# A two-layer decoder trunk on one core: all heads in each step of the recurrence, and the key projection moved between the steps

## Chip, cores and metric

One Trainium2 chip, one core. The metric is the device time of one execution in microseconds (us). Engines: TensorE (PE, its weight loads PEld), VectorE (DVE), ScalarE (ACT), GpSimd (POOL) and SyncE (SP), whose queue issues most of the DMA transfers.

## What is computed

A residual stream of 2048 tokens by 1024 channels passes an RWKV-7 layer (layer A, 16 heads of 64), then one shared key and value projection, then a dilated attention layer (layer B). Cut to what matters here:

```
xr = xr + gate * rwkv7(modulated(rms(xr)))            # layer A: wkv7 state, one per head
kv = rms(xr, kv_norm_g) @ w_kv                        # D -> 2D
k_sh = rope(rms(kv[..., :D] per head, k_norm_g)); v_sh = kv[..., D:]
h = rms(xr, b_norm_g) * (1 + scale) + shift           # layer B's modulated input
q (3 groups), gate = h @ w_in                         # D -> 4D
xr = xr + gate_b * (attention(rope(rms(q)), k_sh, v_sh) * silu(gate)) @ w_out
```

with the state of a head, per token: `state = state*w + (state·a) b^T + v k^T`, `y = state·r`.

## The kernel before, in words

Matrices are multiplied to f32 accuracy in three passes (`mm3`, L68 to 76): both operands are split into a high and a low f32r half, and high·high, high·low and low·high are accumulated. So a projection matmul is three instructions, on L72, L73 and L74.

`phase1` (to 1084 us) computes layer A's projections and writes what the recurrence needs to scratch in HBM. `phase2` (L797 to 1180) runs the recurrence in 32 chunks of 64 tokens. `loads` (L847) fetches a chunk's operands on SP's queue; `prep` (L869) makes the next chunk's matrices on TensorE (L881, L894, L903, L910) with evacuations on ACT and DVE; `chain` (L930) is the serial part. It has three matmul steps with an evacuation behind each: L942 (with L944, a part of the output `y`), evacuated to `qc` by `evac` (L925); L959, evacuated into the state tile `x`; L965 (with L967, the rest of `y`), which DVE scales (`up`, L973) and adds (L976) to make the next chunk's state. A chunk's 16 heads go in two halves `hb`, each a generator of its own, and the loop over chunks (L1150 on) calls the two in turn, so that one half's matmuls stand where the other half's evacuation runs. The L-numbers of these lines are those of the profile; a source matmul in f32 shows as two records there.

Work that fills the time between the steps is kept in a list `work` and advanced by `slot` (L1128): each of a chunk's ten slots advances `prep`, the group norm of the chunk before, and one yield of `work` (two from chunk 24 on if more than one is queued). `work` holds the output projection `out_proj` (L1056) of a block of 256 tokens (every four chunks): 192 matmuls of 256 columns, layer A's result `x1T` to HBM, its sum of squares, and at the end (L1093 to 1096) `rstd1`, the reciprocal root that the norms of the shared key/value and of layer B use. `spread` ties each filler matmul behind the `LAG`-th last mark of the recurrence, `yielding` the DVE work likewise (`DLAG`); the rest of the order is set by a scheduler.

`phase3` runs dense jobs in the order of `JOBS`: `k`, `v`, the queries `2`, `1`, `0`, then `gate` and `out`. A job is 256 places of three matmuls of 512 columns (8 token blocks, 2 halves, 2 groups of 128 tokens, 8 pieces of the contraction). `tokens` (L1296) loads a piece of `x1T` and splits it; in job `v` it also makes layer B's modulated input (`rstd`, L1317, `modulated`) and writes it to `xbT`, which the query jobs read. `rotated` (L1448) norms and rotates keys or queries (`rms_rope`, L1198), transposes them (L1457) and stores them, the keys twice (`K1` and `K2`). Attention starts behind job `2` (`tick(256 * 3 + 14)`).

## Time and profile before

| | us |
|---|---|
| median of 3 runs (3877.28 to 3890.25) | 3888.3 |
| the profiled execution | 3889.0 |
| its span, first to last instruction | 3887.1 |
| recurrence, first to last step | 1086 to 1839 |
| rest of layer A's output projection | 1839 to 1896 |
| jobs `k`, `v`, `2` | 1896 to 2122, to 2313, to 2522 |
| rest (queries 1 and 0, gate, attention, output) | 2522 to 3887 |

TensorE is busy 3700.6 us of the span (95%), DVE 2494.7, ACT 1822.1, POOL 1430.8; the mean granted TensorE clock is 0.962 of full speed. A busy TensorE is one with a matmul in flight, not one at its peak: how densely matmuls start is read from the timeline, from start to start.

### The profile page before, as it was taken

The page shows a single profiled execution, that of the slowest core. Times are in us where ns is not written, and L with a number is a line of the kernel's source. Part 1 is how long each engine was busy: PE and PEld are TensorE (multiplying, and loading weights), DVE is VectorE, ACT ScalarE, POOL GpSimd, SP SyncE. Part 2 cuts the span into 40 slices and gives each one's busy share as a digit, 9 for nine tenths or more (in the row PEclk, how much of TensorE's full clock was granted, in tenths as well). Part 3 has the DMA queues.
Part 4 walks back from the last instruction along what each step waited for, and adds up shares of the span by engine and source line. Part 5 has one row for each costly group of instructions (what it writes and reads, how often), then busy time and mean ns, then how long its engine had stood idle before and what let it go on. Part 6 is the DMA issues. An engine that isn't in the chain of part 4 may idle for free.

```text
span 3887.1 us, 79932 instructions
## 1 busy us (share of the span) xinstructions
PE 3700.6 (95%) x29328; PEld 2930.5 (75%) x29328; DVE 2494.7 (64%) x6213; ACT 1822.1 (47%) x4734; POOL 1430.8 (37%) x1377
## 2 busy tenths in 40 slices
PE   7899999999989999999898999999999999999999
PEld 5565667767777888888776877777777788887888
DVE  4884477889866565465576347777876664455556
ACT  4554443343334443344444233456666665565441
POOL 3341355564344343333344234533432220023232
PEclk9899999999979998899999999999999999999999
DMA  9774467675665443343578455665655565456655
GB/s 279 224 242 138 131 181 205 175 211 163 175 134 124 99 111 90 89 109 92 135 124 167 138 160 79 118 144 144 183 149 136 134 171 138 148 168 193 188 165 174
DMA packets 1027128, 595.31 MB, mean 153 GB/s; under 512 B 564912, under 2 KB 918576, under 8 KB 1020592
## 3 DMA queue, kind: packets, MB, share of 16 engines
q1 hardware_dynamic: 629040, 500.00, 46.1%
q10 hardware_dynamic: 397696, 90.20, 11.1%
q8 instruction: 232, 3.80, 0.4%
q14 instruction: 160, 1.31, 0.1%
HBM read 391.84 MB, written 198.18 MB: 152 GB/s over the span
## 4 chain that ended last, share of the span: by engine, by line
PE 69%; DVE 12%; DMA 7%; issue 4%; POOL 4%; ACT 2%; SPq 1%; ACTq 0%; DVEq 0%; POOLq 0%
PE ps L72 12%; PE ps L74 11%; PE ps L73 11%; PE sc L1640 4%; PE z L881 4%; PE pv L1672 4%; PE z L1661 3%; PE pd L72 2%; PE pd L73 2%; DVE q L1215 2%; PE pd L74 1%; POOL rr_st L1207 1%; DMA bk<-bkD 1%; PE z L269 1%; PE ps L942 1%
## 5 line engine op out<-in xcount | busy, mean ns | idle before, releaser
L1652 ACT ACTIVATE yt<-yt,nm 128x256 f32<-128x256 f32 (+1 forms) x768 | 345.1, 450 | 294.6 <-DVE nm L1648 293.8
L72 PE MATMUL ps<-xh,wh 128*128 128x512 f32 (+1 forms) x1248 | 449.7, 369 | 7.2 <-ACT xh L358 5.6
L73 PE MATMUL ps<-xl,wh 128*128 128x512 f32 (+1 forms) x1248 | 448.0, 360 | 5.4 <-DVE xl L360 4.0
L74 PE MATMUL ps<-xh,wl 128*128 128x512 f32 (+1 forms) x1248 | 445.1, 358 | 0.0
L72 PE MATMUL ps<-xh 128*128 128x512 f32 (+1 forms) x1152 | 419.1, 364 | 4.3 <-ACT ov L1485 2.8
L74 PE MATMUL ps<-xh,xl 128*128 128x512 f32 (+1 forms) x1152 | 400.4, 348 | 0.0
L73 PE MATMUL ps<-xl,xh 128*128 128x512 f32 (+1 forms) x1152 | 398.5, 346 | 0.0
L1207 POOL TENSOR_TENSOR rr_st<-rr_st,mh 128x8 f32<-128x8 f32 x128 | 215.6, 1684 | 469.6 <-DVE rr_st L1206 411.4
L74 PE MATMUL ps<-wh,xl 128*128 128x512 f32 x896 | 362.8, 407 | 14.4 <-DVE xl L66 13.8
L72 PE MATMUL ps<-wh,xh 128*128 128x512 f32 x896 | 370.8, 415 | 4.8 <-ACT q L1450 1.7
L73 PE MATMUL ps<-wl,xh 128*128 128x512 f32 x896 | 361.2, 403 | 0.7 <-DVE wl L1286 0.6
L72 PEld LDWEIGHTS ps<-xh,wh 128*128 128x128 f32 x1248 | 238.9, 193 | 81.3 <-issue 35.8
L1645 DVE CUSTOM_DVE_ANT_0 yt<-sc,amask 128x256 f32<-128x256 f32 (+1 forms) x768 | 237.2, 360 | 86.6 <-PE sc L1640 80.5
L73 PEld LDWEIGHTS ps<-xl,wh 128*128 128x128 f32 x1248 | 240.3, 193 | 60.7 <-issue 18.2
L74 PEld LDWEIGHTS ps<-xh,wl 128*128 128x128 f32 x1248 | 240.4, 193 | 51.6 <-issue 22.2
L72 PEld LDWEIGHTS ps<-xh 128*128 128x128 f32 x1152 | 218.0, 189 | 50.9 <-issue 19.0
L74 PEld LDWEIGHTS ps<-xh,xl 128*128 128x128 f32 x1152 | 217.8, 189 | 27.7 <-issue 0.3
L73 PEld LDWEIGHTS ps<-xl,xh 128*128 128x128 f32 x1152 | 218.5, 190 | 23.0 <-issue 0.3
L1212 POOL TENSOR_TENSOR rr_a<-rr_sq,TCS 128x512 f32<-128x512 f32 x128 | 183.4, 1433 | 114.4 <-DVE rr_sq L1210 98.0
L278 DVE SCALAR_TENSOR_TENSOR t<-hx,vecs,t 128x512 f32<-128x512 f32 x192 | 170.5, 908 | 81.9 <-ACT t L277 81.6
L1215 DVE TENSOR_TENSOR q<-rr_sq,TCS 128x256 f32<-128x256 f32 x256 | 219.7, 898 | 2.6
L74 PEld LDWEIGHTS ps<-wh,xl 128*128 128x128 f32 x896 | 172.0, 192 | 63.9 <-DVE xl L66 26.3
(341 smaller groups left out, 8830.7 us busy)
## 6 DMA issues: line engine op xcount, KB each, us to landing
hx<-hT SPq DMA_DIRECT2D x152, 256.5 KB
xb<-xbT SPq DMA_DIRECT2D x256, 128.0 KB
x<-Q SPq DMA_DIRECT2D x96, 256.0 KB
kq<-K SPq DMA_DIRECT2D x72, 256.0 KB
st<-in_w_in SPq DMA_DIRECT2D x64, 256.0 KB
arD<-ar SPq DMA_DIRECT2D x32, 512.0 KB
bkD<-bk SPq DMA_DIRECT2D x32, 512.0 KB
ls<-arD SPq DMA_DIRECT2D x64, 256.0 KB
```

The lines of the kernel that those rows point to most:

```text
L72: i = mm(out, lh, rh, start=first, stop=False, **kw)
L73: mm(out, lh, rl, start=False, stop=False, **kw)
L74: mm(out, ll, rh, start=False, stop=last, **kw)
L278: nc.vector.scalar_tensor_tensor(t1, hx[:, 0:512], self.vec["a_mix_mu"][:, m:m + 1], t1, op0=ALU.mult, op1=ALU.add)
L881: mm(at[s][:, j], bk[rows[s], 4 * hb + j].rearrange("p a t -> p (a t)"), ls1[b][rows[s], s, 4 * hb + j].rearrange("p a t -> p (a t)"), sta ...
L1207: nc.gpsimd.tensor_tensor(st[:, 1], st[:, 0], mh, op=ALU.pow)
L1212: nc.gpsimd.tensor_tensor(a, sq, TC[:, tt, None, :].to_broadcast([P, 8, 64]), op=ALU.mult)
L1215: nc.vector.tensor_tensor(v[:, :, lo:lo + 32], sq[:, :, hi:hi + 32], TS[:, tt, None, lo:lo + 32].to_broadcast([P, 8, 32]), op=ALU.mult)
L1640: j = mm(sc[h][:, x, :u.n * P], qt[r, c], kq[r, k1 - u.n * P:k1], start=True, stop=True)
L1645: nc.vector.tensor_tensor_reduce(out=u.pr[:, h, :nk], in0=sc[h][:, x, :nk], in1=amask[:, int(g == 0), 256 - nk:256], scale=1.0, scalar=-3e ...
L1652: nc.scalar.activation(u.pr[:, h, :nk], u.pr[:, h, :nk], AF.Exp, bias=nm[:, x, h:h + 1], accum_out=lm[:, x, h, 0:1])
L1672: prev[0] = self.after(mm(pv[e, u.i], u.vt[:, u.i + 2 - u.n + kb, e], u.pts[:, h, kb], start=(kb == 0), stop=(kb == u.n - 1)), prev[0])
```

## The change

The chain takes all heads in each step, in one PSUM bank for each; the two generators become one. The chunk keeps ten slots, now behind the four yields of `SLOTS`, and each advances `work` by two yields (three late). Behind each block's `out_proj`, `keys(v)` is queued: it loads the block's `x1T` back, makes the modulated input and writes it to `xbT` (scale on POOL, affine on ACT), and makes the raw key projection, which goes to `kraw`. Block 0 splits the key weights and stores both halves in `wkD`; blocks 1 to 7 load both halves from there, 32 transfers of 256 KB each. `phase3` loses job `k`; the keys are loaded from `kraw` and rotated in job `v`, and `tokens` no longer modulates. The operand tile `bk` gets a second buffer.

```diff
-LAG = 3
-DLAG = 4
+LAG = 2
+DLAG = 2
...
+SLOTS = (3, 3, 3, 1)
...
+        self.xbT = self.scratch("xbT", (D, T))
+        self.kraw = self.scratch("kraw", (T, D))
+        wkD = self.scratch("wkD", (2 * KC, 2, P, 512))
...
-            bp, ep, lp, kp = pool("bp", 1, cctx), pool("ep", 1, cctx), pool("lp", 2, cctx), pool("kp", 1, cctx)
+            bp, ep, lp, kp = pool("bp", 2, cctx), pool("ep", 1, cctx), pool("lp", 2, cctx), pool("kp", 1, cctx)
...
-            for n, bufs in (("wst", 2), ("dp", 1), ("op", 2)):
+            for n, bufs in (("wst", 2), ("dp", 1), ("op", 2), ("wk", 3)):
...
-            def chain(ch, hb, ls2, yc):
+            def chain(ch, ls2, yc):
...
-                h = slice(4 * hb, 4 * hb + 4)
-                hd = [(s, 4 * hb + j) for j in range(4) for s in range(2)]
+                hd = [(s, j) for j in range(KC) for s in range(2)]
...
+                bank = lambda: pc.tile([P, KC, 64], F32, name="ps")
+                ps, y = bank(), py.tile([P, KC, 64], F32, name="y")
...
                 for s, j in hd:
-                    mm(ps[rows[s], 0, j - 4 * hb], ls1[b][:, s, j, 0], xt[:, s, j], start=True, stop=True)
+                    mm(ps[rows[s], j], ls1[b][:, s, j, 0], xt[:, s, j], start=True, stop=True)
                 for s, j in hd:
-                    i = mm(y[rows[s], j - 4 * hb], ls1[b][:, s, j, 1], xt[:, s, j], start=first[s] is None,
+                    i = mm(y[rows[s], j], ls1[b][:, s, j, 1], xt[:, s, j], start=first[s] is None,
                            stop=False, skip_group_check=True)
...
-                qc = kp.tile([P, 4, 64], F32, name="qc%d" % hb)
-                evac([qc[:, 0:2], qc[:, 2:4]], [ps[:, 0, 0:2], ps[:, 0, 2:4]])
...
+                qc = kp.tile([P, KC, 64], F32, name="qc")
+                evac([qc[:, 0:4], qc[:, 4:8]], [ps[:, 0:4], ps[:, 4:8]])
...
+                yield
+                ps = bank()
                 for s, j in hd:
-                    i = mm(ps[rows[s], 1, j - 4 * hb], tf[b][rows[s], j], qc[rows[s], j - 4 * hb], start=True, stop=True)
+                    i = mm(ps[rows[s], j], tf[b][rows[s], j], qc[rows[s], j], start=True, stop=True)
                 marks.append(i)
...
+                evac([xt[rows[s], s] for s in range(2)], [ps[rows[s]] for s in range(2)])
+                yield
...
-                        up_ = kp.tile([P, 4, 64], F32, name="up")
-                        nc.vector.tensor_tensor(up_, ps[:, 0], pc_, op=ALU.mult)
+                        up_ = kp.tile([P, KC, 64], F32, name="up")
+                        nc.vector.tensor_tensor(up_, ps, pc_, op=ALU.mult)
...
+                work.insert(1, (now[0], keys(v)))
+
+            kvg = self.vec["kv_norm_g"]
+
+            def key_weight(v, i):
+
+                wh, wl = (late["wk"].tile([P, 512], F32R, name="wk" + x) for x in "hl")
+                if v:
+                    for x, t in enumerate((wh, wl)):
+                        nc.sync.dma_start(t.bitcast(F32), wkD[i, x])
+                    return lambda: (wh, wl)
+                kc, c = i % KC, i // KC * 512
+                st = late["wst"].tile([P, 512], F32, name="wst")
+                nc.sync.dma_start(st, ap["w_kv"][kc * P:(kc + 1) * P, c:c + 512])
+
+                def use():
+                    g = kvg[:, kc:kc + 1]
+                    nc.scalar.activation(wh, st, AF.Copy, scale=g)
+                    nc.vector.scalar_tensor_tensor(wl, st, g, wh.bitcast(F32), op0=ALU.mult, op1=ALU.subtract)
+                    for x, t in enumerate((wh, wl)):
+                        nc.sync.dma_start(wkD[i, x], t.bitcast(F32))
+                    return wh, wl
+                return use
+
+            def keys(v):
+
+                t0 = v * 256
+                xh = late["dp"].tile([P, KC, 2, P], F32R, name="yh").rearrange("p k i t -> p k (i t)")
+                xl = late["dp"].tile([P, KC, 2, P], F32R, name="yl").rearrange("p k i t -> p k (i t)")
+                uses = [key_weight(v, i) for i in range(2)]
+                for kc in range(0, KC, 4):
+                    nc.sync.dma_start(xl[:, kc:kc + 4].bitcast(F32),
+                                      self.x1T[kc * P:kc * P + 512, t0:t0 + 256].rearrange("(k p) t -> p k t", p=P))
+                yield
+                yield
+                yield
+                rp = late["pd"].tile([P, 512], F32, name="pd")[:, 0:256]
+                for i in range(2):
+                    mm(rp[:, i * P:i * P + P], self.rstd1[:, 2 * v + i:2 * v + i + 1].to_broadcast([P, P]), self.ident,
+                       start=True, stop=True)
+                rb = late["dp"].tile([P, 256], F32, name="acc")
+                nc.scalar.activation(rb, rp, AF.Copy)
+                yield
+
+                def modulated(kc, x):
+
+                    nc.scalar.activation(x, x, AF.Identity, scale=self.gsB[:, kc:kc + 1], bias=self.adaB[:, kc:kc + 1])
+                    nc.sync.dma_start(self.xbT[kc * P:kc * P + P, t0:t0 + 256], x)
+
+                behind = []
+                for kc in range(0, KC, 2):
+                    q = slice(kc, kc + 2)
+                    raw = xl[:, q].bitcast(F32)
+                    for k in (kc, kc + 1):
+                        x = late["op"].tile([P, 256], F32, name="sq")
+                        nc.gpsimd.tensor_tensor(x, xl[:, k].bitcast(F32), rb, op=ALU.mult)
+                        behind.append((k, x))
+                    nc.scalar.activation(xh[:, q], raw, AF.Copy)
+                    yielding(nc.vector.tensor_sub(xl[:, q], raw, xh[:, q].bitcast(F32)))
+                    yield
+                    for b in behind:
+                        modulated(*b)
+                    behind.clear()
+                for half in range(2):
+                    ps = [late["pd"].tile([P, 512], F32, name="pd") for _ in range(2)]
+                    for kc in range(KC):
+                        i = half * KC + kc
+                        w = uses.pop(0)()
+                        if i + 2 < 2 * KC:
+                            uses.append(key_weight(v, i + 2))
+                        for b in range(2):
+                            c = slice(b * P, b * P + P)
+                            spread(self.mm3(ps[b], (xh[:, kc, c], xl[:, kc, c]), w, kc == 0, kc == KC - 1))
+                            yield
+                    for b in range(2):
+                        o = late["wst"].tile([P, 512], F32, name="wst")
+                        nc.scalar.activation(o, ps[b], AF.Copy, scale=self.rstd1[:, 2 * v + b:2 * v + b + 1])
+                        nc.sync.dma_start(self.kraw[t0 + b * P:t0 + b * P + P, half * 512:half * 512 + 512], o)
+                    yield
 
 
...
-                fill(2 if len(work) > 1 and ch >= RUSH else 1)
+                fill(3 if len(work) > 1 and ch >= RUSH else 2)
...
-                a, b = (chain(ch, hb, ls, yc) for hb in range(2))
-                for i, g in enumerate((a, behind, a, behind, a, b, a, b, a, b)):
-                    next(g, None)
-                    if i == 3 and ch:
+                steps = chain(ch, ls, yc)
+                for i, n in enumerate(SLOTS):
+                    next(steps)
+                    if i == 0 and ch:
                         for _ in gn:
                             pass
                         gn = normed(ch - 1, ylast)
-                    slot(i, ch)
+                    for k in range(n):
+                        slot(k, ch)
                 for _ in pre:
                     pass
-                behind, ylast = b, yc
-            for _ in behind:
-                pass
+                ylast = yc
...
-            JOBS = ("k", "v", 2, 1, 0, "gate", "out")
-            GATE, OUT = 5, 6
...
+            JOBS = ("v", 2, 1, 0, "gate", "out")
...
-                if p == 1 and kc % 2:
-                    xb = two("yp")[:, 0]
-                else:
-                    xb = xb_.tile([P, 256], F32, name="xb")
-                nc.sync.dma_start(xb, (self.x1T if p < 2 else xbT)[rows, sl])
...
-                def modulated():
-                    nc.vector.tensor_scalar(xb, xb, self.gsB[:, kc:kc + 1], self.adaB[:, kc:kc + 1],
-                                        op0=ALU.mult, op1=ALU.add)
-                    nc.scalar.dma_start(xbT[rows, sl], xb)
-                return use
...
-            def rstd(tb):
-
...
-                rb[tb] = two("zp")[:, 0]
-                nc.scalar.activation(rb[tb], rp.rearrange("p a b -> p (a b)"), AF.Copy)
+                xb = xb_.tile([P, 256], F32, name="xb")
+                nc.sync.dma_start(xb, (self.x1T if p == 0 else xbT)[rows, sl])
+
+                return lambda: halves(xb)
...
-            def rotated(job, tt, half, ps, scale):
+            def rotated(job, tt, half, ps):
                 q = s3.tile([P, 8, 64], F32, name="q")
-                nc.scalar.activation(q, ps.rearrange("p (h c) -> p h c", c=64), AF.Copy, scale=scale)
+                if job == "k":
+                    nc.sync.dma_start(q, self.kraw[tt * P:tt * P + P, half * 512:half * 512 + 512].rearrange(
+                        "t (h c) -> t h c", c=64))
+                    for _ in range(4):
+                        yield
+                else:
+                    nc.scalar.activation(q, ps.rearrange("p (h c) -> p h c", c=64), AF.Copy)
...
-                        if s == 0 and (p, tb) >= (0, 7) and (p, tb) < (1, 7):
-                            rstd((tb + 1) % 8)
...
+                        if job == "v" and kc == 0:
+                            after.append(rotated("k", tb * 2 + i, half, None))
...
-            tick(256 * 3 + 14)
+            tick(256 * 2 + 14)
```

**How the order moves.** On TensorE, between two blocks of the output projection, there stood before (L942 and L944 first step, L959 second, L965 and L967 third, L881 matrices of the next chunk, L1024 transposes of the output):

```order
L942 MATMUL ps<-x,ls_1_10362 64x64 x3
L881 MATMUL z<-ls_0_10355,bk 128x128 x4
L942 MATMUL ps<-x,ls_1_10362 64x64 x5
L944 MATMUL y<-x,ls_1_10362 64x64 x4
L881 MATMUL z<-ls_0_10355,bk 128x128 x4
L944 MATMUL y<-x,ls_1_10362 64x64 x4
L965 MATMUL ps<-x,ls_18267 64x64 x7
L1024 MATMUL z<-cst,zc 128x128 x4
L965 MATMUL ps<-x,ls_18267 64x64
L967 MATMUL y<-x,ls_18267 64x64 x8
L959 MATMUL ps<-qc_18778,tf_10366 64x64 x3
L1024 MATMUL z<-cst,zc 128x128 x4
```

and now stands, in the same place of a block (the changed kernel's lines: steps L946 and L948, L963, L970 and L972; matrices L885; transposes L1029; L1098 is the block's sum of squares):

```order
L946 MATMUL ps<-x,ls_1_10368 64x64 x16
L948 MATMUL y<-x,ls_1_10368 64x64 x16
L885 MATMUL z<-ls_0_10361,bk 128x128 x8
L963 MATMUL ps<-qc,tf_10372 64x64 x16
L1098 MATMUL pd<-ones,acc 128x2 x2
L1029 MATMUL z<-cst,zc 128x128 x4
L970 MATMUL ps<-x,ls_15404 64x64
L972 MATMUL y<-x,ls_15404 64x64
L885 MATMUL z<-ls_0_10361,bk 128x128 x4
L970 MATMUL ps<-x,ls_15404 64x64 x10
```

Steps of eight matmuls from two halves became steps of sixteen, with the next chunk's matrices between them and no work of another half.

Farther on in the block, where key matmuls (`pd` from `wkh`, `wkl`; L73 to L75 are the three passes) stand between the steps, there is now on TensorE:

```order
L948 MATMUL y<-x,ls_0_10361 64x64 x2
L885 MATMUL z<-ls_1_10368,bk 128x128 x4
L963 MATMUL ps<-qc,tf_10365 64x64 x4
L75 MATMUL pd<-wkh,yl 128x512 x2
L885 MATMUL z<-ls_1_10368,bk 128x128 x4
L73 MATMUL pd<-wkh,yh 128x512
L74 MATMUL pd<-wkl,yh 128x512
```

Such runs of key matmuls are new; the same places of a chunk held output projection or nothing.

On SP's queue, in the same stretch of a block, the loads of the next chunk (`bk`, `x`, `ls`) now stand among the key weights' loads (L1111) and the stores of the modulated input (L1149):

```order
L856 DMA bk<-bkD 64x8x128
L1111 DMA wkh<-wkD 128x512
L859 DMA bk<-bkD 64x8x64
L1111 DMA wkl<-wkD 128x512
L1111 DMA wkh<-wkD 128x512
L1111 DMA wkl<-wkD 128x512
L859 DMA bk<-bkD 64x8x64
L1149 DMA xbT<-sq 128x256
L869 DMA x<-vP 64x512
L854 DMA ls_0_10361<-arD 64x8x128 x2
L869 DMA x<-vP 64x512
L1111 DMA wkh<-wkD 128x512
```

The last piece of `bk` stands behind four key weights, the state's operands `ls` behind it.

## Rows read from the trace of the kernel before

**Rows 1.** Windows by stage: steps, rest of layer A, jobs `k`, `v` and `2`
```profile
core 0: us, PE busy (x) PEld busy (x) DVE busy (x) ACT busy (x) POOL busy (x), PEclk, DMA share, GB/s
1086.00:1839.00 753.00, 720.24 (x10180) 628.08 (x10179) 438.41 (x1337) 312.32 (x860) 291.53 (x329) 0.91 0.45 103
1839.00:1896.00 57.00, 45.99 (x296) 39.87 (x292) 27.90 (x62) 23.38 (x49) 13.01 (x14) 0.92 0.53 162
1896.00:2122.00 226.00, 204.07 (x904) 160.65 (x905) 162.68 (x287) 105.65 (x210) 109.61 (x75) 0.96 0.70 132
2122.00:2313.00 191.00, 185.33 (x793) 149.84 (x792) 73.06 (x129) 57.53 (x121) 53.29 (x63) 0.97 0.54 163
2313.00:2522.00 209.00, 198.26 (x893) 154.57 (x892) 155.66 (x261) 86.15 (x175) 109.95 (x71) 0.99 0.56 95
```
**Rows 2.** Sources: first and last start of the first and last matmuls of the steps, and values
```profile
L942 PE MATMUL ps<-x,ls x1024: 222/222/369, 1086.4 to 1829.0; 128*64 128x64 f32 x171
L967 PE MATMUL y<-x,ls x1024: 222/222/368, 1103.6 to 1839.0; 128*64 128x64 f32 x171
L1485 ACT ACTIVATE ov<-ps,rstd x32: 670/688/691, 2121.1 to 2306.1; 128x512 f32<-128x512 f32 x32
```
**Rows 3.** Groups by form on TensorE within the steps; last column: idle before, and releasers
```profile
L881 PE MATMUL z<-ls,bk 64*128 64x128 f32 x1003 | 163.9, 314 | 28.0 <-DMA bk<-bkD 16.1 <-issue 10.9 <-PE ps L965 0.7
L72 PE MATMUL pd<-yh,xh 128*128 128x256 f32 x224 | 69.3, 314 | 0.0
L72 PE MATMUL pd<-yh,wh 128*128 128x256 f32 x213 | 68.5, 322 | 0.0
L72 PE MATMUL pd<-xh,wh 128*128 128x512 f32 x25 | 13.4, 535 | 0.0
```
**Rows 4.** Timeline: start, length, instruction; three instructions of a step with work between
```profile
1561.23 0.28 PE L73 MATMUL pd<-yl,wh 128*128 128x256 f32 x1
1561.35 0.28 PE L74 MATMUL pd<-yh,wl 128*128 128x256 f32 x1
1561.56 0.68 PE L959 MATMUL ps<-qc,tf 64*64 64x64 f32 x16
```
**Rows 5.** Timeline in job `v`: three consecutive matmuls of 512 columns
```profile
2181.01 0.39 PE L73 MATMUL ps<-xl,xh 128*128 128x512 f32 x1
2181.25 0.39 PE L74 MATMUL ps<-xh,xl 128*128 128x512 f32 x1
2181.47 0.39 PE L72 MATMUL ps<-xh 128*128 128x512 f32 x1
```
**Rows 6.** Windows within the steps: one with output projection, one without (columns of rows 1)
```profile
1406.00:1448.00 42.00, 41.95 (x606) 36.93 (x600) 25.73 (x75) 19.30 (x55) 18.01 (x20) 1.00 0.45 101
1589.00:1610.00 21.00, 20.60 (x190) 17.89 (x192) 9.40 (x37) 6.04 (x18) 7.88 (x9) 0.52 0.28 62
```
**Rows 7.** Waits of TensorE in the steps, then in the rest of layer A
```profile
PE z L881 <- DMA bk<-bkD: 16.1, 13, 2.2
PE z L881 <- issue: 10.9, 7, 2.7
...
PE pd L1093 <- POOL acc L1088: 5.4, 2, 5.1
```
**Rows 8.** DMA from 20 to 300 us, early in the first stage
```profile
DMA packets 65485, 67.88 MB, mean 242 GB/s; under 512 B 5680, under 2 KB 43701, under 8 KB 65468
...
q1 hardware_dynamic: 57980, 54.04, 65.7%
q10 hardware_dynamic: 7488, 13.63, 13.3%
```
**Rows 9.** Groups by form on VectorE within the steps: evacuations of one half's steps, and a split (L1065)
```profile
L976 DVE TENSOR_TENSOR x<-up,xp 64x256 f32<-64x256 f32 x120 | 53.4, 445 | 2.8
L928 DVE COPY x<-ps 64x256 f32<-64x256 f32 x64 | 27.3, 428 | 50.2 <-ACT x L927 49.0
L973 DVE TENSOR_TENSOR up<-ps,pch 128x256 f32<-128x256 f32 x60 | 25.2, 419 | 47.5 <-PE ps L965 47.3
L1065 DVE TENSOR_TENSOR yl<-yt,yh 128x512 fp32r<-128x512 f32 x28 | 19.7, 720 | 0.8 <-ACT yh L1064 0.4
L928 DVE COPY qc<-ps 128x128 f32<-128x128 f32 x64 | 18.3, 286 | 29.8 <-ACT qc L927 29.5
```
**Rows 10.** Groups from 1880 to 2400 us: the scale of the modulated input, a piece
```profile
L1317 POOL TENSOR_TENSOR yc<-yc,zc 128x256 f32<-128x256 f32 x32 | 26.8, 837 | 128.7 <-DVE xl L66 119.2 <-DMA xbT<-xb 6.9 <-DMA K<-sg 2.6
```

59 lines of the change are left out of this document (25 added, 34 removed).

## The prediction

> **What bounds the kernel now.** I read the windows by stage first [rows 1]. TensorE is busy 720 of 753 us in the recurrence and nearly always in the dense jobs, so no other engine is near its end there (DVE 438, ACT 312, POOL 292 of 753). The question is what TensorE does with its time. The step lines give the stage's borders: the first step starts at 1086.4, the last matmul of the steps at 1839.0 [rows 2]; the values' evacuation shows where job `v` lies.
>
> A busy TensorE is not a full one, so I took the recurrence apart by counts and start-to-start times. The output projection's matmuls of 256 columns within the steps are 224 + 213 per pass, three passes: 1311 [rows 3]. They start 0.12 us apart; where the form changes, from a projection matmul to a step's, the next start is 0.21 us off, so a change of form costs 0.09 [rows 4]. 512 columns take 0.23 [rows 5]. Then 753 us are 1311 x 0.12 = 157 for the projection, 75 x 0.23 = 17 for the last gate matmuls, 9% or 68 us lost to a granted clock of 0.91, and 511 us, 16.0 a chunk, for the recurrence's own matmuls with their waits. The clock has two levels, 1.2 and 2.4 GHz: over a stretch with output projection between the steps it stood at 1.00, in one without at 0.52 [rows 6]; it falls after TensorE did only small matmuls. Of waits the trace names little: 16.1 us for `bk` by DMA and 10.9 before the same matmuls without a releaser [rows 7].
>
> So the steps leave little that is empty, and filler mostly lengthens a chunk. What makes the change pay, if it does, is the other end: jobs `k` and `v` took 226 and 191 us, though job `2`, with the same matmuls, rotation and transposes as `k`, took 209 [rows 1].
>
> **The change, term by term**, against the profiled execution's 3889.0 us (0.7 above the median of the runs).
>
> *Key matmuls between the steps.* There are 768 of 512 columns (8 blocks x 2 halves x 8 pieces x 2 groups x 3). By the order 580 stand before the last step and 188 behind it, and 34 more projection matmuls come before it. 580 x 0.23 + 34 x 0.12 = +138.
>
> *All heads in a step.* The order has 1010 runs of one form before between first and last step, and 835 after: 175 x 0.09 = -16.
>
> *Clock.* More chunks have projection work between their steps, but each block keeps a chunk without any, the order shows. The loss lies between 23 us (if only the first chunks stay slow) and 78 (the old 9% on a longer stage); I take 56, near the old 68, since the bare chunk is there in both orders: -12.
>
> *`bk` in two buffers.* Its loads no longer wait for the transposes of the chunk before: -16, between 0 and -27 [rows 7]; the end without a releaser I leave out.
>
> *Key weights from HBM.* Blocks 1 to 7 load 112 pairs of 256 KB, with three pairs of buffers. SP's queue now has the next chunk's `bk`, `x` and `ls` behind weight loads that wait for a buffer: a late pair stops TensorE, and the steps with it. The trace has no such load; the nearest row is `bk`, 16.1 us in 13 waits, 1.24 each. So between 0 and 112 x 1.24 = 139. Traffic: 67.9 MB at 242 GB/s took 79% of the 16 DMA engines early in stage one [rows 8], so a full share is about 306 GB/s. The change adds 112 x 0.52 = 59 MB of weights, 25 MB for the reload of `x1T`, `xbT` and `kraw`, and 13 for block 0: 97 MB, 317 us of full share on 45% of 753 = 339. That is 656 of about 875 us, but nearly all the new part lies in half of the chunks, where it comes close to full. I take 0.25 us a pair, nearer the lower end since a pair has two others' matmuls to land behind: +28.
>
> *Evacuations.* A step of all heads doubles what a row of one half evacuates: 0.29, 0.43, then 0.42 + 2 x 0.45 us [rows 9]. The old cover, the other half's matmuls, is gone; the new one is the next chunk's matrices and the filler. In the 13 chunks without filler (5 at the start, 8 blocks) three handovers of about 1 us could show: between -20 and +39; I take 0, since the order has matrices and `y` matmuls behind each step there. The rest of a key block, 8 scales of 0.84 us on POOL [rows 10], 4 splits of 0.72 on DVE [rows 9] and as much on ACT, lies beside TensorE: 6.7 us of POOL in some 108 a block, where POOL is busy 39%. If that cover failed, only `xbT` would be late, and nothing reads it before job `2`.
>
> Sum in the steps: 138 - 16 - 12 - 16 + 28 = +122.
>
> *Rest of layer A.* Behind the last step stand now 188 x 0.23 + 192 x 0.12 = 66 us of matmuls against 57 us for the whole stage before. Block 7 adds a serial piece: sum of squares (5.4 us of waiting on POOL [rows 7]), reload of `x1T`, split; I take 10, and 5 for the clock: 81, +24; between +9 and +39.
>
> *Jobs.* `k` and `v` together, 417 us, become a `v` with the key rotation beside it. Its matmuls, transposes and DVE work are those of job `2`; the value evacuation takes the place of the query's. 209, between 202 (matmuls and transposes alone) and the 226 of job `k`: -208. The scattered stores of the keys, DMA at 0.70 in job `k`, set the upper end.
>
> **Forecast:** 122 + 24 - 208 = -62, 3827 us for the profiled execution, 3826 for the median. Its own range goes from no weight waits and 23 us less lost to the clock (-51: 3775) to twice the weight waits and jobs 10 us worse (+38: 3864).
>
> **Rivals.** *The idle of TensorE takes the key work in.* PEld, the weight loads that accompany every matmul, are busy 628 of 753 us, so 125 us would be free; of 138 us only 13 would show, and the sum is 13 + 24 - 208 = -171, 3718. Against it: filler at 1.00 clock and filler-free chunks already differ by the filler's own time. The Trainium skill states the rule, that headroom of TensorE is judged by the weight loads' busy share and not by matmul busy time (Perfetto Trace Analysis, Identifying the Most-Contended Engine); by it the sum would be that 3718, and the trace's 0.09 us for each change of form, with neither in a weight load, speaks against it here. Chance 0.10, and 0.06 for something between this and the forecast.
>
> *Key weights come late.* The place is the first matmul of each pair, in blocks 1 to 7. At the price of `bk`, 1.24 us a pair, the term is 139 instead of 28: +49, 3938. It decides from (62 + 28) / 112 = 0.80 us a pair on; above that the change loses. For it speaks the DMA load in the keyed chunks and the queue's order; against it three pairs of buffers. Chance 0.14.
>
> *The chain shows.* Evacuations cost the full 39 us and the clock keeps its 9% (78 instead of 56 lost): +61, near 3888, no change. For it: nothing of a second half stands behind a step; against it: the matrices do. Chance 0.12.
>
> That job `k` stays is excluded: the order has no key matmuls in `phase3`.
>
> **Chances and range.** The forecast has 0.58. A measurement of this kernel can tell 0.3%, about 12 us, from no change. Faster by more: forecast, the first rival, what lies between, and a few hundredths of the chain's case, 0.76; same: most of the chain's case, 0.09; slower: late weights and the chain's far side, 0.15. The range, 3745 to 3905, leaves out the first rival's end and the half of late weights above 3905.
>
> **What would show it.** Right: the steps take some 875 us instead of 753 while their clock stays near 0.92; weight waits on TensorE's key matmuls sum to about 28 us; the rest of layer A about 81; job `v` about 209 with rotation in it. The steps under 800 us would show the first rival; waits for `wkD` above 90 us the second; waits of step matmuls on `evac` and the adds, and half clock in whole chunks, the third. The forecast is wrong if job `v` takes more than 230 us or the rest of the kernel, 2522 to 3887 before, changes its length.

## The result, and the profile after

The changed kernel takes 3876.2 us (median of 20 runs, 3859.7 to 3888.8) beside 3899.7 for the kernel before on the same chip: ratio 0.993, 95% interval [0.992, 0.995]. That is 23 us (by the medians) to 26 us (by the ratio) faster, where 62 were forecast. On a second chip it took 3863.2 beside 3899.7, ratio 0.990 [0.986, 0.993]. The execution that the first trace shows took 3888.8 us, the longest of its 20; so I took a second trace (3863, the run `e1` below), and read both.

Windows by stage of the changed kernel, first trace (columns of [rows 1]): steps, rest of layer A, job `v`, job `2`.

```profile
1093.50:1963.50 870.00, 818.40 (x10828) 689.86 (x10828) 472.21 (x1220) 368.27 (x890) 323.20 (x321) 0.91 0.69 178
1963.50:2080.00 116.50, 92.53 (x428) 72.88 (x425) 31.16 (x68) 38.17 (x73) 20.53 (x25) 0.87 0.74 237
2080.00:2286.80 206.80, 191.07 (x854) 148.78 (x855) 144.21 (x251) 90.91 (x188) 94.57 (x65) 0.99 0.90 199
2286.80:2504.90 218.10, 200.50 (x898) 158.37 (x896) 157.38 (x263) 87.59 (x180) 110.01 (x71) 0.97 0.67 117
```

The same of its second trace, job `2` in two pieces:

```profile
1087.80:1946.10 858.30, 805.02 (x10827) 680.51 (x10828) 473.32 (x1219) 368.19 (x890) 322.38 (x321) 0.93 0.70 180
1946.10:2060.50 114.40, 90.51 (x430) 70.05 (x427) 31.36 (x69) 38.20 (x73) 20.49 (x25) 0.91 0.76 242
...
2060.50:2263.70 203.20, 189.57 (x854) 147.95 (x855) 143.07 (x250) 91.01 (x187) 94.88 (x64) 1.00 0.95 201
2263.70:2306.00 42.30, 31.82 (x116) 23.71 (x115) 29.05 (x44) 17.80 (x38) 19.30 (x13) 0.80 1.12 233
2306.00:2482.30 176.30, 169.75 (x783) 135.25 (x781) 129.36 (x220) 69.62 (x143) 90.84 (x59) 1.00 0.56 90
```

Beside [rows 1]: the steps took 858 to 870 us instead of 753, as forecast (875). The rest of layer A took 114 to 117, forecast 81. Job `v` took 203 to 207 with the rotation in it, as forecast, but then job `2` took 218. For the kernel before I had set the jobs' borders by the values' evacuation [rows 2]. Counted by their 256 matmuls of the first pass, job `2` ran from 2302.5 to 2505.1 there, 203 us and not 209, and `k` and `v` together 406, not 417. Windows of the kernel before by these borders, `k`, `v`, then job `2` in two pieces:

```profile
1896.30:2088.00 191.70, 185.31 (x837) 146.82 (x837) 137.56 (x245) 90.58 (x180) 93.60 (x62) 0.99 0.67 124
2088.00:2302.50 214.50, 193.59 (x812) 155.01 (x813) 93.78 (x165) 66.83 (x139) 65.78 (x73) 0.94 0.57 160
2302.50:2345.00 42.50, 41.44 (x188) 33.26 (x186) 26.21 (x47) 17.93 (x36) 19.85 (x13) 1.00 0.52 129
2345.00:2505.10 160.10, 153.62 (x700) 119.96 (x698) 118.07 (x199) 64.53 (x134) 82.35 (x53) 1.00 0.56 89
```

From job `1` to the end both kernels take the same (1382 and 1382 in the first pair of traces), so nothing behind job `2` matters.

Waits of TensorE in the changed kernel's steps, first trace (total us, times, longest):

```profile
PE pd L75 <- DVE yl L1160: 13.3, 6, 3.6
PE pd L1140 <- POOL rstd L1101: 5.4, 3, 2.5
PE ps L970 <- ACT x L931: 5.0, 3, 2.5
PE ps L963 <- ACT qc L931: 4.1, 4, 1.6
PE pd L73 <- DMA wkh<-wkD: 3.9, 5, 1.7
```

And in the rest of layer A:

```profile
PE pd L75 <- DVE yl L1160: 7.4, 6, 2.4
PE pd L73 <- DMA wkh<-wkD: 6.7, 5, 2.4
PE pd L1098 <- POOL acc L1093: 3.8, 1, 3.8
```

The waits for `bk` [rows 7] are gone. New are those of the key work: the split of the block loaded back (`yl`), the reciprocal roots, the weights. By these rows the forecast looks right in the steps and short behind them. The experiments show what the steps' total hides.

### The profile page after: what moved, and what is told of

It reads as the page before. It is cut to its first block, busy times and chain, and to the rows that moved or that the text cites. A ratio compares the mean times of both kernels' runs of the same rounds, so it can differ in the third digit from the quotient of the medians.

```text
span 3887.0 us, 79883 instructions
## 1 busy us (share of the span) xinstructions
PE 3671.1 (94%) x29328; PEld 2883.0 (74%) x29328; DVE 2459.5 (63%) x5959; ACT 1831.9 (47%) x4670; POOL 1412.5 (36%) x1317
## 5 line engine op out<-in xcount | busy, mean ns | idle before, releaser
L73 PE MATMUL ps<-xh,wh 128*128 128x512 f32 (+1 forms) x1248 | 451.0, 371 | 10.6 <-ACT xh L359 9.0
L75 PE MATMUL ps<-xh,wl 128*128 128x512 f32 (+1 forms) x1248 | 446.1, 359 | 0.0
L73 PE MATMUL ps<-xh 128*128 128x512 f32 (+1 forms) x1024 | 367.4, 359 | 2.8 <-ACT ov L1555 2.7
L74 PE MATMUL ps<-xl,xh 128*128 128x512 f32 (+1 forms) x1024 | 348.7, 340 | 5.0 <-DVE xl L1375 2.6
L75 PE MATMUL ps<-xh,xl 128*128 128x512 f32 (+1 forms) x1024 | 349.3, 341 | 0.0
L73 PE MATMUL ps<-wh,xh 128*128 128x512 f32 x768 | 321.5, 419 | 9.7 <-ACT xh L66 7.3
L75 PE MATMUL ps<-wh,xl 128*128 128x512 f32 x768 | 312.6, 409 | 12.1 <-DVE xl L67 11.9
L74 PE MATMUL ps<-wl,xh 128*128 128x512 f32 x768 | 312.0, 407 | 0.0
L73 PEld LDWEIGHTS ps<-xh,wh 128*128 128x128 f32 x1248 | 239.5, 194 | 84.0 <-issue 36.6
L75 PEld LDWEIGHTS ps<-xh,wl 128*128 128x128 f32 x1248 | 241.7, 194 | 51.9 <-issue 22.2
L73 PEld LDWEIGHTS ps<-xh 128*128 128x128 f32 x1024 | 193.9, 189 | 42.9 <-issue 19.0
L1293 DVE TENSOR_TENSOR rr_sq<-q,rr_st 128x512 f32<-128x512 f32 x128 | 121.8, 951 | 147.3 <-POOL rr_st L1290 146.5
L74 PEld LDWEIGHTS ps<-xl,xh 128*128 128x128 f32 x1024 | 194.6, 190 | 23.2 <-DVE xl L1375 3.4
L75 PEld LDWEIGHTS ps<-xh,xl 128*128 128x128 f32 x1024 | 194.0, 189 | 21.8 <-issue 0.3
L1709 PE MATMUL sc<-kq,x 64*128 64x256 f32 (+1 forms) x1536 | 204.2, 360 | 4.6 <-DVE lm L1714 4.4
```

What stands on the lines that cost most here:

```text
L73: i = mm(out, lh, rh, start=first, stop=False, **kw)
L74: mm(out, lh, rl, start=False, stop=False, **kw)
L75: mm(out, ll, rh, start=False, stop=last, **kw)
L1293: nc.vector.tensor_tensor(sq, v, st[:, 1].unsqueeze(2).to_broadcast([P, 8, 64]), op=ALU.mult)
L1709: j = mm(sc[h][:, x, :u.n * P], qt[r, c], kq[r, k1 - u.n * P:k1], start=True, stop=True)
```

## The experiments

The kernel before was timed beside each group of runs, its median between 3893.6 and 3906.8, so between groups ratios are compared rather than times.

**The two parts apart.** `e1` is the changed kernel again. `e2` is the kernel before with the recurrence of the change alone: its `chain`, its loop with `SLOTS`, `LAG` and `DLAG` of 2, and two buffers for `bk`; the filler keeps its rate.

```diff
-LAG = 3
-DLAG = 4
+LAG = 2
+DLAG = 2
...
-            def chain(ch, hb, ls2, yc):
+            def chain(ch, ls2, yc):
```

`e3` is the changed kernel with just these parts undone; `keys` and job `v` stay as changed.

> The changed kernel as it is, for a second trace: its first one was of an execution of 3888.8 us, 12.6 above the median. If what it showed is the kernel's own, the steps again take about 870 us, the rest of layer A 116, job v 207 and job 2 218, and the time beside the kernel before is 0.993. If the first trace's extra time was the granted clock alone (0.956, 0.960 to 0.966 in other runs), the same waits come back and the stages with long matmuls in them are shorter by 12 us together, 7 of them in the first stage, which the change does not touch.

> The kernel before with all heads in each step and two buffers for bk alone; the keys stay a job of their own. By the prediction's terms (-16 fewer forms, -12 clock, -16 bk) the steps take 709 us instead of 753 and the time is 3856, ratio 0.989. By the rival that the chain shows (evacuations +39, clock unchanged) it is -16 - 16 + 39 = +7, ratio 1.002. By the first trace of the changed kernel (bk and its issue waits 26 us less, 11 us of new evacuation waits, clock unchanged) -16 - 26 + 11 = -31, ratio 0.992.

> The changed kernel with the recurrence of before (two halves, one buffer for bk): the key projection and the modulated input between the steps alone. If the two parts add, its ratio is 0.993 divided by that of the chain alone: 1.001 if the chain gives 31 us, 1.004 if it gives the predicted 44. By the prediction's terms (138 + 28 in the steps, 24 behind, 208 off the jobs) -18, ratio 0.995. If the key work needs the all-head steps to find room, it is worse than 1.01, with waits for bk above 30 us in the steps.

Measured: `e1` 0.990 [0.986, 0.993]; `e2` **0.965** [0.962, 0.969], 3766.7 us; `e3` 1.003 [1.001, 1.006]. No theory had it: without the key work the recurrence's part is worth 133 us, and the key work, in either recurrence, costs. Added to the kernel before it costs 14 us (`e3`), added to `e2` 97. Steps of `e3` with its rest of layer A:

```profile
1088.50:2001.10 912.60, 858.32 (x10822) 707.12 (x10823) 485.84 (x1378) 379.63 (x984) 336.29 (x379) 0.92 0.66 170
2001.10:2119.00 117.90, 92.50 (x433) 71.46 (x429) 31.50 (x65) 38.55 (x75) 22.45 (x27) 0.88 0.74 233
```

Steps of `e2`:

```profile
1085.60:1722.80 637.20, 624.47 (x10160) 560.27 (x10160) 432.45 (x1173) 298.61 (x761) 279.38 (x267) 0.96 0.55 122
```

Against the steps of before (753 us, TensorE busy 720, clock 0.91 [rows 1]) idle time (length less busy) falls from 33 to 13, and what the clock loses (one less the granted clock, times the length) from 68 to 25. Some 50 us of the 116 are neither.

**Which of it: the buffer or the heads.** `e5` is the kernel before with one character changed, `e6` is `e2` with that character back at 1, `e11` is `e5` with two buffers for the small tiles (`kp`) too.

```diff
-            bp, ep, lp, kp = pool("bp", 1, cctx), pool("ep", 1, cctx), pool("lp", 2, cctx), pool("kp", 1, cctx)
+            bp, ep, lp, kp = pool("bp", 2, cctx), pool("ep", 1, cctx), pool("lp", 2, cctx), pool("kp", 1, cctx)
```

> The kernel before with a second buffer for bk and nothing else. All heads in a step with two buffers took the steps from 753 to 637 us: 42 us less lost to the granted clock, 20 less of idle TensorE, 52 less in the recurrence's own matmuls. If bk gives only its waits (16.1 + 10.9 us named in the trace of before): -16 to -27, ratio 0.993 to 0.996. If those waits are also what lets the clock fall: -27 - 42 = -69, ratio 0.982. If TensorE only meets the next late operand sooner: ratio 1.000.

> All heads in each step, but one buffer for bk; the keys a job of their own. If the merged halves carry most of the gain and bk its waits alone: 3767 plus 16 to 27, ratio 0.969 to 0.972, with waits for bk of 16 us or more. If the clock hangs on the waits for bk: 3767 + 69 = 3836, ratio 0.983, with some 70 us lost to the clock in the steps again. If bk hardly matters with merged halves, since its transposes stand further from the loads: 0.965.

> The kernel before with two buffers for bk, and two for the pool of the chain's and the matrices' small tiles (kp: qc, xp, up, ot, t). If single buffers bind the order in the same way as bk did, the steps fall below 610 us and the ratio below 0.963. If bk was the only one that bound, 0.967.

| | two halves | all heads |
|---|---|---|
| keys a job, one `bk` | 1 | 0.991 [0.988, 0.994] (`e6`) |
| keys a job, two `bk` | **0.967** [0.964, 0.969] (`e5`) | 0.965 [0.962, 0.969] (`e2`) |
| keys in the steps, one `bk` | 1.003 [1.001, 1.006] (`e3`) | not run |
| keys in the steps, two `bk` | 0.993 [0.990, 0.995] (`e13`) | 0.990 and 0.993 (changed) |

The second buffer alone gives 130 us (3763.3, `e11` no more: 0.965 [0.962, 0.968]), nearly five times the 27 us of waits that the trace named for it. Beside the key work the same buffer gives 41 us (`e3` to `e13`, by the ratios), so its worth and the cost of the key work are not separate terms. All heads in a step give 35 us without the buffer and nothing beside it. Steps of `e5`, and in them a stretch of 14 us with next to no projection work (three matmuls):

```profile
1084.30:1708.70 624.40, 615.85 (x10181) 543.05 (x10181) 447.22 (x1334) 310.03 (x858) 301.86 (x327) 0.97 0.54 125
...
1576.70:1590.90 14.20, 13.71 (x283) 12.06 (x282) 13.69 (x45) 6.82 (x18) 7.67 (x9) 1.00 0.62 132
```

Such a stretch of the kernel before, the one of [rows 6] by its borders:

```profile
1585.10:1606.40 21.30, 19.07 (x203) 16.78 (x202) 10.78 (x36) 7.03 (x21) 7.80 (x9) 0.61 0.33 78
```

So 24 of the 129 us that the steps lose are idle time (33 to 9) and 49 are clock (68 to 19). The projection matmuls lie in a block's eight half chunks as before: 42 (now 40), five times 30, then none or nearly none in two. But in the two bare ones TensorE hardly waits any more (0.5 us of the 14.2, against 2.2 of the 21.3, one wait for `bk`), and the granted clock is 1.00, its level of 2.4 GHz. Most of the rest stands in one row, the matmuls behind `bk` (L881, 163.9 us busy in [rows 3]), 68 us less, a part of it the clock's:

```profile
L881 PE MATMUL z<-ls,bk 64*128 64x128 f32 x1000 | 95.8, 288 | 1.8 <-DVE mv L992 1.4 <-ACT qc L927 0.2
```

The timeline shows how. In the kernel before (the profile counts each of these matmuls twice):

```profile
1643.97 1.16 PE L881 MATMUL z<-ls,bk 64*128 64x128 f32 x8
...
1645.87 1.16 PE L881 MATMUL z<-ls,bk 64*128 64x128 f32 x8
```

With two buffers:

```profile
1614.04 1.16 PE L881 MATMUL z<-ls,bk 64*128 64x128 f32 x16
```

Eight matmuls of 64 rows take the 1.16 us that four took, with projection matmuls 0.12 us apart, so at the same clock, beside both. The program writes them for the upper and the lower 64 rows in turn (`rows[s]`). With one buffer the scheduler's order tears them apart, four and then, behind other work, four: by the trace's records 117 of this line's 122 unbroken runs are such fours, and 27 of 77 in `e5`. That each four is of one half is read from the pace; the profile names no half. That the scheduler does so because the two halves of `bk` come by different transfers is likely, but no run here tries it alone.

**The order by itself.** `e9` is the kernel before with the turn held by the edit below; `e10` is `e5` with the same edit, but the loops over `s` and `j` exchanged.

```diff
+                    prev = None
                     for j in range(4):
                         for s in range(2):
-                            mm(at[s][:, j], bk[rows[s], 4 * hb + j].rearrange("p a t -> p (a t)"),
+                            prev = self.after(mm(
+                               at[s][:, j], bk[rows[s], 4 * hb + j].rearrange("p a t -> p (a t)"),
```

> The kernel before with one buffer for bk, and its L881 matmuls held in the order in which the program writes them: the two row halves of the array (s = 0 and 1) in turn. In the trace of before they run 8 in 1.16 us, one half's after the other's; with a second buffer 16 in 1.16 us. If it is this order that costs, L881's mean from start to start falls from 122 to about 77 ns, the steps by 1024 x 45 ns = 46 us while the idle time (33) and the clock's loss (69) stay: ratio 0.988. If the second buffer's gain is in the loads and the clock, or the turn makes the first half's matmuls wait for the second half's loads: 1.000 or above.

> The kernel before with two buffers for bk, its L881 matmuls held in the other order: all four of one row half, then all of the other. If running the halves in turn is worth what the own time of the recurrence shows, the steps rise from 624 by 46 to 70 us while idle time and clock loss stay at 9 and 21: time 3763 + 46 to 70, ratio 0.978 to 0.985. If the order within these groups does not matter: 0.967.

Measured: `e9` 0.994 [0.992, 0.996], `e10` 0.971 [0.967, 0.974]. Steps and the group of `e9`:

```profile
1088.40:1823.30 734.90, 672.20 (x10181) 582.13 (x10182) 436.68 (x1334) 312.10 (x859) 295.26 (x327) 0.92 0.48 106
```

```profile
L882 PE MATMUL z<-ls,bk 64*128 64x128 f32 x1008 | 112.1, 312 | 29.2 <-DMA bk<-bkD 18.3 <-issue 6.8 <-DVE ls L890 2.0
```

and of `e10`, with one of its groups on the timeline:

```profile
1083.30:1741.50 658.20, 641.32 (x10177) 570.57 (x10177) 462.32 (x1335) 309.14 (x859) 296.63 (x328) 0.96 0.51 118
```

```profile
L882 PE MATMUL z<-ls,bk 64*128 64x128 f32 x1000 | 120.3, 295 | 1.4 <-DVE ls L890 1.4
```

```profile
1606.57 1.71 PE L882 MATMUL z<-ls,bk 64*128 64x128 f32 x16
```

In `e9` TensorE's busy time falls by 48 us and that of the group by 52, as the theory of the turn says; but the idle time rises from 33 to 63, and only 18 us of the steps are won. The held matmuls themselves wait no longer than before (29.2 us, before 28.0); those behind them do, above all the first step, for `ls`:

```profile
L944 PE MATMUL ps<-x,ls 128*64 128x64 f32 x1024 | 62.2, 241 | 14.3 <-DVE ls L888 13.5 <-DVE x L978 0.6
```

In `e10` four and four side by side take 1.71 us, the group 120 instead of 96 us and the steps 34 more. The run takes 16 us more than `e5` by the ratios, whose intervals overlap, and 23 more than `e11` on the same chip, under the 46 to 70 that I expected: neighbouring halves still overlap in part. So the turn is real, some 50 us of TensorE's busy time in `e9` and 24 in `e10`'s group, and held by force without the buffer it gives back most of it as waits. That the torn order was the scheduler's way around the late load fits this, but is not shown. Nor is the turn the whole of the 130 us: in `e2`, with two buffers, 72 of 101 runs are still fours and the group is busy for 123.5 us, 28 more than in `e5`, yet the run takes no longer. How much of the gain is the clock's and how much the waits', no run separates.

```profile
L882 PE MATMUL z<-ls,bk 64*128 64x128 f32 x1000 | 123.5, 291 | 4.9 <-ACT ls L914 2.5 <-DVE ls L889 1.5 <-issue 0.6
```

**All heads beside the key work.** `e13` is `e3` with `pool("bp", 2, cctx)`.

> The key work between the steps, the recurrence in two halves as before, and two buffers for bk: the changed kernel without the all-head steps. With the keys a job of their own the all-head steps were worth nothing once bk had two buffers (3767 against 3763). If that holds beside the key work too, this takes the time of the changed kernel, ratio 0.990 to 0.993, steps about 858. If the all-head steps are what lets the key work in, it is slower, 1.000 or more. If two halves cover each other's evacuations in the chunks that have little filler, it is faster, below 0.985, with steps under 840.

Measured 0.993 [0.990, 0.995], the changed kernel's time without its all-head steps. Its steps are 57 us shorter than those of `e3`:

```profile
1085.80:1941.70 855.90, 820.21 (x10823) 679.22 (x10823) 490.94 (x1379) 378.60 (x986) 338.82 (x381) 0.93 0.69 181
```

**What the key work costs.** `e7` takes away the serial piece between a block's output projection and its key matmuls: `keys` gets the projection's tiles, has no reload and no split, and makes `rb` behind its first half and the modulated input in its second.

```diff
-                work.insert(1, (now[0], keys(v)))
+                work.insert(1, (now[0], keys(v, yh, yl)))
```

`e8` takes away the weights' loads, `e14` both.

```diff
                 if v:
-                    for x, t in enumerate((wh, wl)):
-                        nc.sync.dma_start(t.bitcast(F32), wkD[i, x])
-                    return lambda: (wh, wl)
+                    return lambda: kept_w[i % len(kept_w)]
```

> The changed kernel without the serial piece between a block's output projection and its key matmuls: the key projection multiplies the split tiles of the output projection, so x1T is neither loaded back nor split again, and the rows' reciprocal roots are needed only after half of the key matmuls. It computes keys and layer B's input of layer A's normalised output instead of x1. The same matmuls, weights, stores and scales. Beside the all-head chain alone the changed kernel's steps take 221 us more: 139 for matmuls, 37 for the clock, 41 idle. If the serial piece leaves the chunks bare, most of the 78 goes: steps about 790 instead of 858, rest of layer A about 95 instead of 114, time 3780, ratio 0.969. If the key matmuls or their weights are dear wherever they stand, the steps stay within 15 us and the ratio is 0.986.

> The changed kernel without the 59 MB of key weights in blocks 1 to 7: these blocks multiply the last three pairs of block 0, which stay where they are (so the keys of these blocks are of other weights). If late weights and DMA traffic make the steps dear (the second rival of the prediction), the steps fall by 40 us or more, ratio 0.978 or less. If they cost only the named waits (about 8 us in the steps, 7 in the rest of layer A), the time falls by 10 to 15 us, ratio 0.986.

> The changed kernel without the serial piece (the key projection multiplies the split tiles of the output projection, as in the run without the piece) and without the key weights' loads in blocks 1 to 7 (their keys are of the last three pairs of block 0). Each alone gave 37 and 42 us. If they are separate costs they add: 3863 - 79 = 3784, steps 798, ratio 0.971. If the weights' waits only take the place of the piece's (18 us of them came up when the piece went) more than the sum: 3770, ratio 0.968. If both only remove the same empty stretches: 3815, ratio 0.981; the rest of the key work's 97 us is then in the filler itself.

Measured: `e7` 0.984 [0.981, 0.987], `e8` 0.983 [0.980, 0.986], `e14` 0.972 [0.970, 0.975]. By the ratios, against the two of the changed kernel (0.990 and 0.993), that is 23 to 37 us less, 28 to 42 and 68 to 82; the 37, 42 and 81 of the medians compare different chips. Steps of `e7`, then of `e8` with its rest of layer A, then of `e14`:

```profile
1093.80:1923.90 830.10, 786.67 (x10849) 662.77 (x10850) 452.49 (x1194) 352.75 (x859) 322.35 (x319) 0.95 0.68 180
```

```profile
1085.50:1911.70 826.20, 790.05 (x10825) 676.63 (x10826) 470.92 (x1218) 367.03 (x887) 324.12 (x320) 0.93 0.53 135
1911.70:2010.90 99.20, 86.39 (x432) 71.11 (x429) 32.43 (x69) 38.77 (x74) 22.93 (x27) 0.90 0.40 125
```

```profile
1087.30:1892.40 805.10, 776.66 (x10868) 666.23 (x10868) 453.60 (x1194) 355.49 (x860) 320.26 (x319) 0.96 0.52 129
```

The two costs add as far as single traces tell: steps and rest of layer A together are shorter than in `e1` by 39 us (`e7`, whose rest takes 104), 47 (`e8`) and 84 (`e14`). Weights: 32 us in the steps (858 to 826) and 15 behind them (114 to 99), where only 6 and 7 us of waits carry the name of their loads. Serial piece: in `e7` the clock's loss falls from 60 to 42 and the idle time from 53 to 43, though without the piece the weights are later, 17.7 us of named waits (`wkh`, from the first step to 1930 us). How the clock stands where the piece lies, this stretch of `e1` shows, between a block's projection and its keys; it holds only 16 key matmuls, and just before it TensorE did small matmuls and waited 1.3 us for `ls` and 0.4 for the sum of squares:

```profile
1718.40:1740.00 21.60, 21.60 (x218) 17.29 (x217) 7.79 (x22) 7.47 (x18) 9.76 (x10) 0.53 0.51 142
```

With neither cost (`e14`) the kernel still takes 0.972 where `e2`, with the keys as a job, takes 0.965: in the steps 168 us more than `e2`, behind them 84 instead of 58, against 187 from the jobs. Of the 168, 16 are idle time and 7 clock, so some 145 go to the 634 further matmuls, for which the prediction's prices give 140. The matmuls themselves eat most of what their job took.

**Behind the steps.** `e12` keeps block 7's pieces of `x1` in tiles that are free by then and splits them in `out_proj` as they are made; the key matmuls then read these pieces, and the roots are made beside them. `e4` stores `K2` in runs of 1 KB (second piece of the diff, for job `k` alone).

```diff
+                    nc.scalar.activation(direct(1, e).bitcast(F32R), t1, AF.Copy)
+                    nc.vector.tensor_sub(direct(2, e).bitcast(F32R), t1, direct(1, e))
...
-                        nc.scalar.dma_start(dst.rearrange("p j (r t i) -> p t (j r) i", r=16, i=16)[:, tt // 2],
-                                            o2.rearrange("p j (r i) -> p (j r) i", r=16))
+                        nc.scalar.dma_start(dst[:, :, tt // 2 * 256:tt // 2 * 256 + 256], o2)
```

> The changed kernel with block 7's keys made without the way over HBM: its pieces of x1 are kept and split as the output projection makes them, in tiles that are free by then, and the reciprocal roots and the modulated input are made beside the key matmuls. If the serial piece behind the last output projection sets the rest of layer A, that falls from 114 to about 95 us (the waits for yl 7.4, acc and rstd 4.8, and some of the clock's 10 to 15), ratio 0.985 beside 0.990 of the changed kernel on one chip and 0.993 on another. If the weights' loads and the late start of job v set it, it stays above 108.

> The changed kernel with the second copy of the keys (K2) stored in the order of the tokens, in runs of 1 KB instead of 64 bytes; the same bytes, so layer B's group 2 works on the keys of other tokens. If the DMA engines' backlog from these stores holds up job 2's first weights and tokens, the DMA share in job v falls from 0.90 to below 0.6, job 2 takes about 203 us instead of 218, job v some 5 us less, and the time falls by 15 to 20 us, ratio 0.988. If it is the rotation's work on POOL, DVE and ACT, both jobs keep their length and the ratio stays 0.993.

`e12` measured 0.989 [0.986, 0.993]; its rest of layer A:

```profile
1953.90:2054.50 100.60, 87.09 (x430) 69.19 (x427) 30.70 (x71) 38.09 (x77) 19.58 (x24) 0.93 0.82 272
```

The stage lost 14 us as the theory has it, with the waits for `yl`, 7.4 us in the first trace, nearly gone (0.3). In the time of the run that can't be told from nothing: its steps came out 7 us longer than those of `e1`, which a single execution can.

`e4` measured 0.988 [0.984, 0.991], 9 us less than `e1` on the same chip, half of what I expected. DMA queue of the stores of keys and values (q10) in job `v`, packets, MB and share of 16 engines, in `e1`:

```profile
q10 hardware_dynamic: 125289, 21.77, 63.4%
```

and in `e4`, with its jobs `v` and `2` (the first 43 us of `2`, then the rest):

```profile
q10 hardware_dynamic: 25440, 21.76, 33.0%
```

```profile
2067.60:2266.40 198.80, 186.39 (x855) 149.15 (x855) 143.31 (x250) 92.22 (x187) 98.22 (x65) 1.00 0.66 211
2266.40:2309.00 42.60, 39.00 (x163) 30.28 (x164) 34.59 (x57) 21.88 (x46) 23.35 (x15) 0.92 0.71 224
2309.00:2477.70 168.70, 160.00 (x734) 126.17 (x732) 122.55 (x208) 64.93 (x133) 87.50 (x56) 1.00 0.57 90
```

The same bytes in a fifth of the packets halve the queue's share. Job `2`'s first 42 us hold 163 matmuls instead of 116, and jobs `v` and `2` take 410 us instead of 422; from the last step to the end of job `2`, where the rest of layer A counts too, 8 us are won. The backlog of 64-byte runs is thus worth 8 to 12 us, the rest of job `2`'s delay is not it.

## Why the forecast was wrong

The sum in the steps, +122, came out at +105 to +117. Behind the last step the sum has 24 - 208 = -184; the two traces have -125 and -130 there (541 and 536 us from the last step to the end of job `2`, before 666). So the miss in the time lies behind the steps, and the steps' total is right, but not by the terms that it was added from. Term by term, in the order buffer first, key work second (single traces, so each to some 10 us):

| term | forecast | measured |
|---|---|---|
| second buffer for `bk` | -16 | **-130** (`e5`) |
| all heads: form changes and clock | -16, -12 | none beside the buffer (`e2`, `e5`) |
| key matmuls in the steps | +138 | by the counts 580 x 0.23 + 54 x 0.12 = +140 |
| late weights in the steps | +28 | +32 (`e8`) |
| further idle time and clock beside the keys | 0 | the remainder, 221 - 140 - 32 = +49 (`e2`, `e1`) |
| rest of layer A | +24 | 114 - 58 = +56 |
| jobs | -208 | 422 - 609 = -187 |

With 221 for the three terms of the key work in the steps the last column sums to -40, beside the -37 of the second chip's medians.

**The step that failed in the time** is the price of what stands behind the last step. *Rest of layer A*: to 66 us of matmuls I added 10 for the serial piece, 5 for the clock and nothing for late weights, 81. `e1` takes 114: 24 of idle time, 10 of clock, and 7 for 30 matmuls of job `v` in this stage (before, 48 of job `k` stood there). Without the way over HBM the stage loses 14 us (`e12`), without the weights' loads 15 (`e8`), without the reload, the split and the loads 31 (`e14`). *Jobs*: 208 rested on borders read from the evacuations; counted borders give 406 - 203 = 203. Of the other 16, the key stores' backlog takes 8 to 12 (`e4`); I had named these stores for the upper end and left them out of the sum. The remaining few us stay open.

**The step with the wrong mechanism** is "`bk` in two buffers": I priced the buffer by the waits that carry its name, 16.1 us with an upper end of 27. What else hung on it stood in the rows that I quoted: the group behind the buffer was busy 163.9 us [rows 3], 68 more than with two buffers, and in the bare chunks the clock stood at 0.52 [rows 6], which I took for a matter of filler, since TensorE did only small matmuls there. It does so in `e5`'s bare stretch too, with hardly a wait, at 1.00. This error alone would have made the change faster than forecast.

**Key work and recurrence are not separate terms**, and so no order of adding them is the true one. Taken with the key work first (`e3`), its steps cost 913 - 753 = +160 where 138 + 28 = 166 were said; the recurrence's part then gives 858.3 - 912.6 = -54 (-43 by the first trace) where -44 was said, all of it the buffer's (-57, `e13`) and none the heads'. Taken with the buffer first, the buffer gives 130 and the key work takes most of it back. In either order the total comes out, and the split does not: that part was luck. Why the buffer is worth less beside the key work is not shown.

**The key work in the steps.** The price of its matmuls holds (`e14`), and so does that of late weights there, 32 us for 28, though only 6 us of waits carry their name where I wrote that 28 would show; with the 15 us behind the steps it is 47 / 112 = 0.42 us a pair, where 0.25 was forecast and the second rival needed 0.80. Not priced was that a block's chain of projection, sum of squares, reload and split leaves stretches with neither filler nor full clock: I let the clock take 56 us in the steps, and it took 60 and 78 in the two traces, where `e2`, without the key work, loses 25.

One slip in the prediction's sums: the low end of its own range takes 23 us less lost to the clock, but from 56 down to its bound of 23 it is 33, so 3765 and not 3775.

The rivals: *the idle of TensorE takes the key work in* is refuted. The steps of `e2` have PEld busy for 560 of 637 us, so 77 free; 140 us of matmuls made them 221 longer. The Trainium skill has the rule that TensorE's headroom is judged by MFU (the share of peak arithmetic) and the weight loads' busy share (Perfetto Trace Analysis, Identifying the Most-Contended Engine). Read as room for filler, the free share would have let only 140 - 77 = 63 us show, and these traces do not agree with that reading. *Key weights come late* had the right place at about a third of its price (0.42 of 1.24 us a pair). *The chain shows* was half right: the clock kept its loss (60 to 78 us, 78 said), the evacuations show 9 us of named waits (39 said). The steps of some 875 us, which I wrote would show the forecast right, came out of terms of other sizes: a sum of terms is not tested by its total.

The kernel before with `bk` in two buffers takes 3763.3 us, 0.967 of before, and is some 100 us faster than the change. `e2` and `e11` (0.965) can't be told from it.

## What to carry to other kernels

Price a single buffer by the operation behind it, not by its waits alone: compare that operation's busy time per instruction with the best that the same rows show elsewhere, and look whether its matmuls run in the order that the program writes. Before bundling a buffer with a restructuring, time it alone, since here one character held more than the whole gain, the rest of the change gave most of it back, and beside that rest the same character was worth a third (41 of 130 us). Moving a dense job into a latency-bound stage pays only for what that stage leaves empty: here a job that was already near TensorE's pace cost its own matmuls again, and the serial piece and the loads that came with it were paid with idle time and with the clock.

## What the runs showed of the hardware

Matmuls of 64 contracted rows on the upper and the lower half of the array run side by side when they stand in turn in TensorE's order: eight in 1.16 us, eight in 1.71 when four of one half stand before four of the other, and 2 x 1.16 when, by their pace, fours of one half stand apart. The Trainium skill says that different tiles of the array can execute weight loads and matmuls in parallel (TensorEngine Tiling (Array Packing), Key Properties); these runs agree, and show that the order of the instructions decides whether it happens. With a third of the bytes of the key and value stores in runs of 64 bytes, their queue took 63.4% of the 16 DMA engines' time in job `v`; with that third in runs of 1 KB the same bytes took 33.0%.
